# The last down projection with tokens split 282 and 238 instead of 260 and 260

## The chip, the core and the metric

One core of a Trainium2 chip. The metric is the device time of one launch in microseconds (us), as the median of several runs. Engines are named as in the profile: PE is TensorE (PEld its weight loads), DVE is VectorE, ACT is ScalarE, POOL is GpSimd, SP is SyncE, which issues most DMAs.

## The reference

One decoder layer for 512 prompt tokens and 8 single sampled tokens, 520 in all, with 1024 features, in fp32: a feed-forward block (2816 hidden units), a mixer of two parallel head groups, a second feed-forward block, and a final norm. Only the end bears on this change:

```python
def _rms_norm(x, g):
    xf = x.astype(jnp.float32)
    y = xf * lax.rsqrt(jnp.mean(xf * xf, axis=-1, keepdims=True) + EPS)
    return (y * g.astype(jnp.float32)).astype(x.dtype)

def _swiglu(x, wg, wu, wd):
    return (jax.nn.silu(x @ wg) * (x @ wu)) @ wd
...
    h = h + 0.5 * _swiglu(_rms_norm(h, ffn2_norm[l]), ffn2_w_gate[l], ffn2_w_up[l], ffn2_w_down[l])
...
    return _rms_norm(h, final_norm), ...
```

## The kernel before

Features lie on the 128 partitions (1024 features are 8 tiles, `KD`), tokens on the free axis: `h` is 128 x 8 x 520. A product is made of three one-pass matmuls: each operand is split into a rounded high part (type fp32r) and a low part, and `mm3` (L150 to L155) adds high x high, high x low and low x high in PSUM.

The second feed-forward block runs in `stream`: hidden tiles 1 to 21 with gate, up and most of the down projection. What is left at the end is the down projection over the last 6 hidden tiles (16 to 21), done by `down_by_half` (L637): for each of 2 halves of the tokens (`HALVES`, 260 each) and each of 8 output tiles d, a unit of 6 x 3 = 18 matmuls into a PSUM tile `dh_db` (tile d, half b). In the first half the last hidden tile comes late, so units 0 to 5 are begun without it and closed together. PSUM tiles come from two rings of two (tag "BE" for even d, "A" for odd d; tiles 2 and 3 of the first half have banks of their own), so unit (0, 1) needs the bank of `dh_40`, that is DVE must have read it.

Behind each unit `done` (L673) runs: DVE makes `th` = -0.5 x `dh` x r (L677; r is the norm's factor) and adds it to `h` (L679). The `th` tiles take turns in three buffers (tag "ac"). Then `after2` (L837) gathers the final norm: ACT squares the new `h`, DVE adds the square to `acc_last` (`sumsq`, L187 to L194), and ACT scales `h` by the gain into `hg` (L851). The squares (`sq_l`) come from another pool, `tmp`.

`finish(0)` makes the first half's norm, while PE works on the second half: one matmul with ones sums `acc_last` over the partitions on all partitions (`psl`, L873), ACT takes square roots in two pieces (`r_last`, L875, for which ACT loads the table of that function), DVE takes reciprocals (L879), then multiplies `hg` by them in four pieces of two tiles (L883), and SP stores each piece (L885). The second half can't hide its norm, so `finish(1)` puts tokens on partitions: squares as weights against a column of ones give the sums of 65 tokens in each of 4 columns (`psl1`, L864), ACT and DVE make root and reciprocal of 65 x 4 values (`r_tok`, L865, L867), PE transposes them back to all partitions (`factor`, L870), and DVE multiplies and SP stores. The last unit's `th`, `h` and squares are cut in two (`QUARTERS`), and the squares of tiles 6 and 7 (`late`) go to the sums without being added up first.

Each engine runs its own program in order. The order is set at build time by a scheduler that simulates the program; some instructions are pinned to the order of the code (`keep_in_program_order`: the reciprocals, the multiplies of L883, the first matmuls of most units of the second half). While the first units close, DVE and ACT also update the states of the sampled tokens (`hs`, `room`, L1193 and L1195).

Of the kernel before, what the change touches and what calls it, by code (L numbers as in the profile page):

```python
# [10 lines left out]
F32 = mybir.dt.float32  # L11
F32R = mybir.dt.float32r
AF = mybir.ActivationFunctionType
ALU = mybir.AluOpType
# [3 lines left out]
P = 128  # L18
# [3 lines left out]
NT = SEQ + NS  # L22
HB = NT // 2
HALVES = (slice(0, HB), slice(HB, NT))
KD = D // P
FFN = 2816
KF = FFN // P
# [41 lines left out]
def tile_trunk_step(ctx: ExitStack, tc: tile.TileContext, ins: dict, outs: dict):  # L69
    nc = tc.nc  # L70
# [79 lines left out]
    def mm3(ps, whi, wlo, xhi, xlo, start, stop, pin=False, **kw):  # L150
        first = nc.tensor.matmul(ps, whi, xhi, start=start, stop=False, **kw)  # L151
# [3 lines left out]
        nc.tensor.matmul(ps, wlo, xhi, start=False, stop=stop, **kw)  # L155
# [11 lines left out]
    def ws(w, k, m=P):  # L167
        return w[:, k * m : (k + 1) * m]
# [15 lines left out]
                                       op0=ALU.mult, op1=ALU.subtract)  # L184
        sumsq(acc, d, hs, name)

    def sumsq(acc, d, hs, name):  # L187
        n = hs.stop - hs.start
        if d == 0:
            nc.scalar.activation(out=acc[:, hs], in_=h[:, d, hs], func=AF.Square)  # L190
        else:
            sq = tmp.tile([P, HB], F32, tag="ta", name=f"sq_{name}_{d}")
            nc.scalar.activation(out=sq[:, :n], in_=h[:, d, hs], func=AF.Square)
            added[:] = [nc.vector.tensor_tensor(out=acc[:, hs], in0=acc[:, hs], in1=sq[:, :n], op=ALU.add).ins]  # L194

# [75 lines left out]
    class Ffn:  # L271
# [367 lines left out]
        def down_by_half(self, c, lo, after, wd):  # L639
            n = KF - lo  # L640
            banks, units = {}, []
            for d in range(KD):
                if d < STATES[2]:
                    next(self.states)
                src, name = ins[f"w{self.i}d"][d, :, lo * P :], f"{self.i}d{d}_{c}"
                raw = raw_tile(name)[:, : n * P]
                nc.sync.dma_start(out=raw, in_=src)
                if d < 4:
                    home = (wp, 3, ("whi", "wlo")) if d < 2 else (self.wx, 2, ("shi", "slo"))
                    units.append(split(raw, n * P, name, *home))  # L650
                    continue
                hi, lw = (wd.tile([P, n * P], F32R, tag=t, bufs=KD - 4, name=f"{t}_{name}") for t in ("dhi", "dlo"))
                nc.scalar.copy(hi, raw)
                nc.vector.tensor_tensor(out=lw, in0=raw, in1=hi.bitcast(F32), op=ALU.subtract)
                units.append((hi, lw))

            def part(d, b, ks):
                if (d, b) not in banks:
                    if b == 0 and d in (2, 3):
                        banks[d, b] = bank(f"dh{self.i}_{d}{b}")  # L660
                    elif d % 2:
                        banks[d, b] = ps[0].tile([P, 512], F32, tag="A", bufs=2, name=f"dh{self.i}_{d}{b}")
                    else:
                        t = ps[0].tile([P, 2, 512], F32, tag="BE", bufs=2, name=f"dh{self.i}_{d}{b}")
                        banks[d, b] = t[:, 0]
                wh, wl = units[d]
                for k in ks:
                    g = self.g[lo + k]
                    mm3(banks[d, b][:, :HB], ws(wh, k), ws(wl, k), g[:, 0, b], g[:, 1, b], k == 0, k == n - 1,
                        pin=b == 1 and k == 0 and d != 1)  # L670

            def done(d, b):
                hs = HALVES[b]  # L673
                t = self.wx.tile([P, 2, HB], F32, tag="ac", bufs=3, name=f"th{self.i}_{d}{b}")[:, 0]
                for c in QUARTERS if (d, b) == (KD - 1, 1) else (slice(0, HB),):
                    cs = slice(hs.start + c.start, hs.start + c.stop)
                    nc.vector.scalar_tensor_tensor(out=t[:, c], in0=banks[d, b][:, c], scalar=-0.5, in1=self.nx[3][:, cs],  # L677
                                                   op0=ALU.mult, op1=ALU.mult)
                    nc.vector.tensor_tensor(out=h[:, d, cs], in0=t[:, c], in1=h[:, d, cs], op=ALU.add)  # L679
# [90 lines left out]
    f2 = {}  # L770
# [49 lines left out]
    def before2():  # L820
        f2["xt"].release()
        f2["hg"] = pool("hg", "right")
        res.append(f2["hg"].tile([P, KD, NT], F32, tag="hg", name="hg"))
        res.append(f2["hg"].tile([P, HB], F32, tag="rl", name="r_last"))
        res.append(f2["hg"].tile([TQ, 4], F32, tag="rt", name="r_tok"))
# [10 lines left out]
    def after2(d, b, hs):  # L836
        hg = res[0]  # L837
        if (d, b) == (0, 1):
            finish(0)
        elif b and todo:  # L840
            todo.pop(0)()
        if b and d == KD - 2:
            square(d, hs)
        elif b and d == KD - 1:
            for c in QUARTERS:
                square(d, slice(hs.start + c.start, hs.start + c.stop))
        else:
            sumsq(last, d, hs, f"l{d}{b}")
        end = (d, b) == (KD - 1, 1)
        with queued(*((finish(1),) if end else ())):  # L850
            nc.scalar.activation(out=hg[:, d, hs], in_=h[:, d, hs], func=AF.Copy, scale=v("final_norm", d))  # L851
        if end:
            while todo:
                todo.pop(0)()

    def finish(b):
        hs, hg, rl, rt, idt = HALVES[b], *res
        acc = last[:, hs]
        if b:
            sums = bank("psl1")[:TQ, :4]  # L860
            for k, sq in enumerate((acc, late[0], None)):
                for q in range(4):
                    s = late[1 + q // 2][:, q % 2 * TQ :][:, :TQ] if sq is None else sq[:, q * TQ : (q + 1) * TQ]
                    nc.tensor.matmul(sums[:, q : q + 1], s, ones[:, :1], start=(k, q) == (0, 0), stop=(k, q) == (2, 3))  # L864
# [3 lines left out]
            factor = bank("factor")[:, :HB]  # L868
            for q in range(4):
                nc.tensor.transpose(factor[:, q * TQ : (q + 1) * TQ], rt[:, q : q + 1].to_broadcast([TQ, P]), idt)  # L870
        else:
            ps = bank(f"psl{b}")[:, :HB]
            nc.tensor.matmul(ps, ones, acc, start=True, stop=True)  # L873
            for c in QUARTERS:
                nc.scalar.activation(out=rl[:, c], in_=ps[:, c], func=AF.Sqrt, bias=eps, scale=1.0 / D)  # L875
            root, factor = None, rl

        def inverse(q):
            tc.keep_in_program_order(nc.vector.reciprocal(out=rl[:, q], in_=rl[:, q]))  # L879

        def out(d, n):
            tc.keep_in_program_order(
                nc.vector.tensor_tensor(out=hg[:, d : d + n, hs], in0=hg[:, d : d + n, hs],  # L883
                                        in1=factor.unsqueeze(1).to_broadcast([P, n, HB]), op=ALU.mult))
            nc.sync.dma_start(out=outs["y"][:, d : d + n, hs], in_=hg[:, d : d + n, hs])  # L885

        if not b:
            todo.extend([lambda q=q: inverse(q) for q in QUARTERS])
# [597 lines left out]
```

## Time and profile before

| | us |
|---|---|
| median of 3 runs | 954.12 (953.4 to 954.48) |
| span of the profiled execution, first to last instruction | 951.9 |
| what the median has beyond that span | 2.2 |
| PE busy in the span | 942.5 (99%) |
| DVE busy | 852.7 (90%) |
| ACT busy | 635.7 (67%) |

Times in rows are us from the span's start. A row in order of time gives the start, how long it was busy, engine, line, operation, what it writes and reads, the shape, and how many such instructions were put together; in square brackets stands how long the engine was idle before it and who ended that. PE's matmuls overlap in the pipe: each is shown with about 0.28 us, though one starts every 0.12 us.

### The profile page before, as it was taken

The numbers are of one execution on the slowest core, as the hardware profiler recorded it, in microseconds if no ns is written. First come the engines' busy times: TensorE is split into PE (matmuls) and PEld (weight loads), VectorE is DVE, ScalarE is ACT, GpSimd is POOL, SyncE is SP. The second block draws the span as 40 slices with busy tenths as digits, with TensorE's granted clock in tenths as the row PEclk, the third lists the DMA queues.
The fourth block names the chain that finished last, engine by engine and source line by source line (L and its number), as shares of the span: only waits on it lengthen the run. The fifth ranks groups of instructions, "written<-read, shape, count | busy, mean of one in ns | idle before, by whom it ended". The sixth has DMA issues, their size and how long they took to land.

```text
span 951.9 us, 19681 instructions
## 1 busy us (share of the span) xinstructions
PE 942.5 (99%) x7674; PEld 925.9 (97%) x7674; DVE 852.7 (90%) x1462; ACT 635.7 (67%) x1179; POOL 148.3 (16%) x230
## 2 busy tenths in 40 slices
PE   9999999999999999999999999999999999999996
PEld 8999999999999999999999999999999999999996
DVE  6899899998988688789998998999999999999886
ACT  7777756677566455485668735777776676766774
POOL 0011100100100000046251100111112101122120
PEclk9999999999999999999999999999999999999998
DMA  7666554455553343354264453556666655776552
GB/s 205 187 166 150 143 151 135 115 140 156 134 155 95 86 134 122 92 180 138 91 184 133 141 114 115 138 122 160 163 173 176 163 146 144 171 194 185 145 180 91
DMA packets 53995, 138.35 MB, mean 145 GB/s; under 512 B 7750, under 2 KB 15878, under 8 KB 53902
## 3 DMA queue, kind: packets, MB, share of 16 engines
q1 hardware_dynamic: 39918, 104.19, 34.2%
q0 software_dynamic: 13712, 32.78, 18.7%
q8 instruction: 60, 0.98, 0.4%
q14 instruction: 33, 0.27, 0.1%
q10 hardware_dynamic: 272, 0.13, 0.0%
HBM read 129.74 MB, written 7.34 MB: 144 GB/s over the span
## 4 chain that ended last, share of the span: by engine, by line
PE 44%; DVE 2%; issue 1%; POOL 1%; DMA 1%; ACT 1%; DVEq 0%; ACTq 0%; POOLq 0%
PE A L160 8%; PE BE L160 6%; PE wo L160 5%; PE A L165 4%; PE BE L165 3%; PE wo L165 2%; PE P L311 1%; PE dh L155 1%; PE dh L151 1%; PE dh L154 1%; POOL zs L1068 1%; PE inz L151 1%; PE inz L154 1%; PE inz L155 1%; DMA room<-in_state_ssm 1%
## 5 line engine op out<-in xcount | busy, mean ns | idle before, releaser
L504 ACT COPY ac<-A 128x260 f32<-128x260 f32 x85 | 31.6, 372 | 35.4 <-PE A L155 17.3
L433 DVE TENSOR_TENSOR s<-raw 128x1024 f32<-128x1024 f32 x39 | 47.6, 1222 | 4.4 <-DMA raw<-in_w2gu 2.8
L504 ACT COPY ac<-BE 128x260 f32<-128x260 f32 x41 | 15.4, 376 | 33.6 <-PE BE L165 17.7
L151 PE MATMUL inx<-xh_mx,whi_inx 128*128 128x260 f32 x112 | 31.8, 284 | 0.0
L154 PE MATMUL inx<-xl_mx,whi_inx 128*128 128x260 f32 x112 | 31.6, 282 | 0.0
L155 PE MATMUL inx<-xh_mx,wlo_inx 128*128 128x260 f32 x112 | 31.6, 282 | 0.0
L1027 DVE SCALAR_TENSOR_TENSOR A<-U,h,A 128x544 f32<-128x544 f32 x36 | 29.0, 807 | 1.6 <-ACT A L1025 1.2
L311 PE MATMUL P<-x,raw 128*128 128x260 f32 x128 | 28.9, 385 | 0.2 <-DMA raw<-in_w1gu 0.2
L311 PEld LDWEIGHTS P<-x,raw 128*128 128x128 f32 x128 | 24.4, 192 | 4.2 <-DMA raw<-in_w1gu 0.6
L160 PE MATMUL wo<-catg,whi_wo 128*128 128x260 f32 x192 | 27.4, 285 | 0.0
L1193 ACT ACTIVATE so<-br,sxdt 128x128 f32<-128x128 f32 x64 | 22.8, 376 | 5.8 <-DVE room L1195 5.2
L160 PEld LDWEIGHTS wo<-catg,whi_wo 128*128 128x128 f32 x192 | 24.8, 188 | 0.2
L139 ACT CAST thi<-raw 128x1024 fp32r<-128x1024 f32 (+1 forms) x14 | 14.2, 1012 | 15.7 <-PE wo L160 4.8
L1304 DVE TENSOR_TENSOR h<-wo,h 128x260 f32<-128x260 f32 x48 | 19.2, 422 | 5.0 <-PE wo L165 4.7
L252 DVE TENSOR_TENSOR gs<-gq,gs 128x780 fp32r<-128x780 f32 (+1 forms) x28 | 23.3, 831 | 0.0
L151 PE MATMUL inz<-xh_mx,whi_inz 128*128 128x260 f32 x80 | 23.0, 287 | 0.0
L154 PE MATMUL inz<-xl_mx,whi_inz 128*128 128x260 f32 x80 | 22.7, 284 | 0.0
L155 PE MATMUL inz<-xh_mx,wlo_inz 128*128 128x260 f32 x80 | 22.6, 283 | 0.0
L251 ACT CAST gs<-gq 128x780 fp32r<-128x780 f32 (+1 forms) x28 | 20.6, 735 | 1.2 <-DVE gq L555 0.8
L151 PEld LDWEIGHTS inx<-xh_mx,whi_inx 128*128 128x128 f32 x112 | 21.1, 188 | 0.2 <-issue 0.2
L160 PE MATMUL A<-xth_f,qs 128*128 128x260 f32 x84 | 21.2, 283 | 0.0
L160 PE MATMUL A<-xtl_f,qs 128*128 128x260 f32 x84 | 21.2, 284 | 0.0
(3140 smaller groups left out, 4382.9 us busy)
## 6 DMA issues: line engine op xcount, KB each, us to landing
raw<-in_w2gu SPq DMA_DIRECT2D x44, 512.0 KB, 4.4
raw<-in_w1gu SPq DMA_DIRECT2D x41, 512.0 KB, 4.3
raw<-in_w_in SPq DMA_DIRECT2D x24, 512.0 KB, 3.7
raw<-in_w1d SPq DMA_DIRECT2D x16, 512.0 KB, 4.6
raw<-in_w2d SPq DMA_DIRECT2D x16, 512.0 KB, 4.6
raw<-in_w_out SPq DMA_DIRECT2D x12, 512.0 KB, 3.5
ab<-scr_acs SPq DMA_DIRECT2D x8, 512.0 KB, 5.5
h<-in_state_ssm SPq DMA_DIRECT2D x16, 256.0 KB, 3.7
```

Of the source, the lines that this page charges most:

```text
L151: first = nc.tensor.matmul(ps, whi, xhi, start=start, stop=False, **kw)
L154: nc.tensor.matmul(ps, whi, xlo, start=False, stop=False, **kw)
L155: nc.tensor.matmul(ps, wlo, xhi, start=False, stop=stop, **kw)
L160: mm = nc.tensor.matmul(ps, w, x, start=start, stop=False, **kw)
L165: nc.tensor.matmul(ps, w, xhi[k], start=False, stop=k == len(wlo) - 1, **kw)
L251: cast = nc.scalar.copy(hi, s)
L252: low = nc.vector.tensor_tensor(out=lo, in0=s, in1=hi.bitcast(F32), op=ALU.subtract)
L311: mm = nc.tensor.matmul(self.banks[f, u][b][:, :HB], ws(self.raw[f][:, u], j + 4 * q), xg[:, slot[q]], start=j == q == 0, stop=j == 3 and ...
L433: nc.vector.tensor_tensor(out=s1, in0=diag, in1=up0, op=ALU.add)
L504: self.copied = nc.scalar.copy(keep, out[:, :HB]).ins
L1027: nc.vector.scalar_tensor_tensor(out=A[:, :n], in0=U[:, j : j + n], scalar=w(j), in1=A[:, :n], op0=ALU.mult, op1=ALU.add)
L1193: nc.scalar.activation(out=o[:, q], in_=br, func=AF.Copy, scale=sxdt[:, j, b : b + 1]))
```

## The change

The tokens of this last stretch are split into `SPANS`, 282 (`WIDE`) and 238 (`NARROW`), instead of halves of 260; all that runs ahead of it keeps its halves. `TQ` becomes 119, so that the second part fills 2 columns of 119 partitions instead of 4 of 65: the last sums are 6 matmuls instead of 12, the transposes 2 instead of 4. A square of 282 tokens doesn't fit `tmp`'s tiles of 260, so the first part's squares move to the ring of three "ac" buffers that the `th` tiles use.

```diff
+WIDE = 282
+NARROW = NT - WIDE
+SPANS = (slice(0, WIDE), slice(WIDE, NT))
...
-TQ = HB // 4
-QUARTERS = slice(0, HB // 2), slice(HB // 2, HB)
+TQ = NARROW // 2
+QUARTERS = slice(0, TQ), slice(TQ, NARROW)
...
-    def sumsq(acc, d, hs, name):
+    def sumsq(acc, d, hs, name, home=tmp, tag="ta"):
...
-            sq = tmp.tile([P, HB], F32, tag="ta", name=f"sq_{name}_{d}")
+            sq = home.tile([P, HB if home is tmp else NT], F32, tag=tag, name=f"sq_{name}_{d}", **({} if home is tmp else {"bufs": 3}))
...
-                    g = self.g[lo + k]
-                    mm3(banks[d, b][:, :HB], ws(wh, k), ws(wl, k), g[:, 0, b], g[:, 1, b], k == 0, k == n - 1,
-                        pin=b == 1 and k == 0 and d != 1)
+                    g = self.g[lo + k].rearrange("p a b t -> p a (b t)")[:, :, SPANS[b]]
+                    pin = b == 1 and k == 0 and d != 1
+                    mm3(banks[d, b][:, : g.shape[-1]], ws(wh, k), ws(wl, k), g[:, 0], g[:, 1], k == 0, k == n - 1, pin)
...
-                hs = HALVES[b]
-                t = self.wx.tile([P, 2, HB], F32, tag="ac", bufs=3, name=f"th{self.i}_{d}{b}")[:, 0]
-                for c in QUARTERS if (d, b) == (KD - 1, 1) else (slice(0, HB),):
+                hs = SPANS[b]
+                t = self.wx.tile([P, 2, HB], F32, tag="ac", bufs=3, name=f"th{self.i}_{d}{b}").rearrange("p b t -> p (b t)")
+                for c in QUARTERS if (d, b) == (KD - 1, 1) else (slice(0, hs.stop - hs.start),):
...
-            sumsq(last, d, hs, f"l{d}{b}")
+            sumsq(last, d, hs, f"l{d}{b}", *(() if b else (f2["wx"], "ac")))
...
-            sums = bank("psl1")[:TQ, :4]
+            sums = bank("psl1")[:TQ, :2]
             for k, sq in enumerate((acc, late[0], None)):
-                for q in range(4):
-                    s = late[1 + q // 2][:, q % 2 * TQ :][:, :TQ] if sq is None else sq[:, q * TQ : (q + 1) * TQ]
-                    nc.tensor.matmul(sums[:, q : q + 1], s, ones[:, :1], start=(k, q) == (0, 0), stop=(k, q) == (2, 3))
+                for q, c in enumerate(QUARTERS):
+                    s = late[1 + q] if sq is None else sq[:, c]
+                    nc.tensor.matmul(sums[:, q : q + 1], s, ones[:, :1], start=(k, q) == (0, 0), stop=(k, q) == (2, 1))
...
-            for q in range(4):
-                nc.tensor.transpose(factor[:, q * TQ : (q + 1) * TQ], rt[:, q : q + 1].to_broadcast([TQ, P]), idt)
+            for q, c in enumerate(QUARTERS):
+                nc.tensor.transpose(factor[:, c], rt[:, q : q + 1].to_broadcast([TQ, P]), idt)
...
-            for c in QUARTERS:
+            for c in parts:
                 nc.scalar.activation(out=rl[:, c], in_=ps[:, c], func=AF.Sqrt, bias=eps, scale=1.0 / D)
```

`parts` cuts the 282 tokens into two of 141; the sizes of `hg`'s multiplies, of `r_last`, `r_tok` and the identity `idt` follow. The number of matmuls of `down_by_half` stays 2 x 8 x 18, and the scheduler orders the stretch anew.

More of the change, by code (lines that the diff above doesn't have):

```diff
@@ L823, in before2 @@
         res.append(f2["hg"].tile([P, KD, NT], F32, tag="hg", name="hg"))
-        res.append(f2["hg"].tile([P, HB], F32, tag="rl", name="r_last"))
-        res.append(f2["hg"].tile([TQ, 4], F32, tag="rt", name="r_tok"))
+        res.append(f2["hg"].tile([P, WIDE], F32, tag="rl", name="r_last"))
+        res.append(f2["hg"].tile([TQ, 2], F32, tag="rt", name="r_tok"))
         res.append(f2["hg"].tile([TQ, TQ], F32, tag="idt", name="idt"))
@@ L867, in finish @@
             tc.keep_in_program_order(nc.vector.reciprocal(out=rt, in_=rt))
-            factor = bank("factor")[:, :HB]
-            for q in range(4):
-                nc.tensor.transpose(factor[:, q * TQ : (q + 1) * TQ], rt[:, q : q + 1].to_broadcast([TQ, P]), idt)
+            factor = bank("factor")[:, :n0]
+            for q, c in enumerate(QUARTERS):
+                nc.tensor.transpose(factor[:, c], rt[:, q : q + 1].to_broadcast([TQ, P]), idt)
         else:
-            ps = bank(f"psl{b}")[:, :HB]
+            ps = bank(f"psl{b}")[:, :n0]
             nc.tensor.matmul(ps, ones, acc, start=True, stop=True)
-            for c in QUARTERS:
+            for c in parts:
                 nc.scalar.activation(out=rl[:, c], in_=ps[:, c], func=AF.Sqrt, bias=eps, scale=1.0 / D)
@@ L883, in out @@
                 nc.vector.tensor_tensor(out=hg[:, d : d + n, hs], in0=hg[:, d : d + n, hs],
-                                        in1=factor.unsqueeze(1).to_broadcast([P, n, HB]), op=ALU.mult))
+                                        in1=factor.unsqueeze(1).to_broadcast([P, n, n0]), op=ALU.mult))
             nc.sync.dma_start(out=outs["y"][:, d : d + n, hs], in_=hg[:, d : d + n, hs])
         if not b:
-            todo.extend([lambda q=q: inverse(q) for q in QUARTERS])
+            todo.extend([lambda q=q: inverse(q) for q in parts])
         spans = [(1, 2), (3, 2), (5, 2), (7, 1)] if b else [(2, 2), (4, 2), (6, 2)]
```

4 lines of the change are left out of this document (3 added, 1 removed).

## The prediction

> **What bounds the kernel now.** I read the page first, then the busy times by stretch, then the end of the chain that ended last, then the rows of TensorE (PE), VectorE (DVE) and ScalarE (ACT) in order of time, from us 918 to the end.
>
> ```profile
> span 951.9 us, 19681 instructions
> PE 942.5 (99%) x7674; PEld 925.9 (97%) x7674; DVE 852.7 (90%) x1462; ACT 635.7 (67%) x1179; POOL 148.3 (16%) x230
> 904.00:925.00 21.00, 21.00 (x177) 21.00 (x176) 17.55 (x44) 14.58 (x35) 6.42 (x12) 1.00 0.62 203
> 925.00:943.00 18.00, 18.00 (x157) 17.94 (x156) 15.89 (x41) 11.40 (x27) 0.00 (x0) 1.00 0.15 51
> 943.00:946.00 3.00, 1.44 (x19) 1.16 (x18) 1.23 (x6) 1.20 (x4) 0.00 (x0) 1.00 0.26 89
> 942.38 0.13 PE dh L155
> 942.54 0.49 DVE th L677 x2
> 945.38 0.43 DVE hg L883
> 946.41 1.55 DVE hg L883 x3
> ```
>
> After the window come its length and the busy time of PE, weight loads, DVE, ACT and POOL, then the granted clock. PE is busy for all of 904 to 943 at full clock, and the chain lies on its matmuls (`dh`) up to 942.5; behind that it is a relay over DVE, ACT and PE, and the store of the output. So the time is lost or won in two ways: by what moves the start of the last `th` (942.54 now), and by the length of the relay behind it. DVE in 925 to 943 has 15.9 of 18 us, so it is a close second.
>
> **The matmuls.** Their pace, and the nearest other shapes:
>
> ```profile
> 920.33 0.28 PE L151 MATMUL dh<-g,dhi_2d 128*128 128x260 f32 x1
> 924.55 0.28 PE L155 MATMUL dh<-g,dlo_2d 128*128 128x260 f32 x1
> 924.67 0.28 PE L151 MATMUL dh<-g,whi_2d 128*128 128x260 f32 x1
> 940.07 0.28 PE L155 MATMUL dh<-g,dlo_2d 128*128 128x260 f32 x1
> 942.22 0.28 PE L155 MATMUL dh<-g,dlo_2d 128*128 128x260 f32 x1
> 19.76 3.23 PE L311 MATMUL P<-x,raw 128*128 128x260 f32 x14
> 429.46 1.02 PE L1259 MATMUL pst<-xw,bt 128*128 128x512 f32 x2
> L311 PE MATMUL P<-x,raw x128: 382/382/594, 4.6 to 34.0; 128*128 128x260 f32 x128
> L1259 PE MATMUL pst<-xw,bt x16: 590/592/595, 429.5 to 533.6; 128*128 128x512 f32 x16
> L957 PEld LDWEIGHTS dt<-xh_mx,whi_w x16: 120/121/123, 351.8 to 355.9; 128*48 128x48 f32 x16
> L956 PEld LDWEIGHTS dt<-xl_mx,whi_w x14: 94/94/98, 352.1 to 355.7; 128*16 128x16 f32 x14
> L165 PEld LDWEIGHTS A<-xth_f,qs x84: 186/188/193, 625.2 to 911.7; 128*128 128x128 f32 x84
> ```
>
> 18 matmuls of one output tile take 942.22 - 940.07 = 2.15 us, 0.1196 each, and 0.1203 in the first half (920.33 to 924.67 for 36). No row has a one-pass matmul of another width than 260. The unsplit fp32 records go on at (3.23 - 0.382)/13 = 0.219 us for 260 columns and at 1.02 - 0.592 = 0.43 for 512, so 0.84 ns per column; I take half of that for the one-pass form (an estimate): 22 columns are 9.2 ns. So 282 columns cost 0.1295 and 238 cost 0.1104: the wide half takes 144 x 0.0092 = 1.3 us more, the narrow one as much less. Bounds: a pace that doesn't depend on the width (0.12 for both), and, for the narrow form, the fp32 rows, two records of 0.219 per matmul at 260, which is 0.40 at 238.
>
> [...]
>
> **What moves in the order.** VectorE's program in the first half of the tokens, from tile `th_20` on (`th` is the scaled down product, `h` the residual sum, `sq_l` a square that ACT makes of that `h`, `acc_last` its running sum), before:
>
> ```order
> L679 TENSOR_TENSOR h<-th_20_11562,h 128x260
> L677 SCALAR_TENSOR_TENSOR th_30_11588<-dh_30_11569,r_f_7261 128x260
> L677 SCALAR_TENSOR_TENSOR th_40_11614<-dh_40_11595,r_f_7261 128x260
> L194 TENSOR_TENSOR acc_last<-acc_last,sq_l_1_11555 128x260
> L677 SCALAR_TENSOR_TENSOR th_50_11640<-dh_50_11621,r_f_7261 128x260
> L679 TENSOR_TENSOR h<-th_30_11588,h 128x260
> ```
>
> and in the change:
>
> ```order
> L197 TENSOR_TENSOR acc_last<-acc_last,sq_l_1_11555 128x282
> L682 TENSOR_TENSOR h<-th_20_11562,h 128x282
> L680 SCALAR_TENSOR_TENSOR th_30_11588<-dh_30_11569,r_f_7261 128x282
> L197 TENSOR_TENSOR acc_last<-acc_last,sq_l_2_11565 128x282
> L682 TENSOR_TENSOR h<-th_30_11588,h 128x282
> L680 SCALAR_TENSOR_TENSOR th_40_11614<-dh_40_11595,r_f_7261 128x282
> ```
>
> The squares of the first half now share three buffers with the `th` tiles, so each `th` stands behind the sum that frees its buffer: `th_40`, which was taken early to free the PSUM tile of `dh_40`, now has two sums of squares, and so two round trips over ACT, ahead of it.
>
> ScalarE's program in the second half, before (the table of the square root, then the roots `r_last` of the first half, stand ahead of the square of tile 3):
>
> ```order
> L193 ACTIVATE sq_l_2_11777<-h 128x260
> L851 ACTIVATE hg<-h 128x260
> L875 ACT_TABLE_LOAD
> L875 ACTIVATE r_last<-psl_11721,eps 128x130 x2
> L193 ACTIVATE sq_l_3_11805<-h 128x260
> ```
>
> and in the change, where both have moved behind that square, and so behind matmuls of one more output tile:
>
> ```order
> L196 ACTIVATE sq_l_2_11777<-h 128x238
> L854 ACTIVATE hg<-h 128x238
> L196 ACTIVATE sq_l_3_11805<-h 128x238
> L880 ACT_TABLE_LOAD
> L880 ACTIVATE r_last<-psl_11721,eps 128x141 x2
> ```
>
> VectorE waits for those roots with two reciprocals that stand ahead of all its other work of tiles 4 to 7, in both programs.
>
> **The first half, by rows.**
>
> ```profile
> 919.01 0.28 PE L155 MATMUL dh<-g,wlo_2d 128*128 128x260 f32 x1
> 919.59 0.76 DVE L677 SCALAR_TENSOR_TENSOR th<-dh,r_f 128x260 f32<-128x260 f32 x2
> 920.86 0.87 DVE L1195 SCALAR_TENSOR_TENSOR hs<-hs,sdec,so 128x128 f32<-128x128 f32 x3
> 923.45 0.76 DVE L677 SCALAR_TENSOR_TENSOR th<-dh,r_f 128x260 f32<-128x260 f32 x2
> 932.04 0.43 DVE L679 TENSOR_TENSOR h<-th,h 128x260 f32<-128x260 f32 x1
> 932.56 0.42 ACT L193 ACTIVATE sq_l<-h 128x260 f32<-128x260 f32 x1 [1.40 <-DVE h L679]
> 933.02 0.43 DVE L194 TENSOR_TENSOR acc_last<-acc_last,sq_l 128x260 f32<-128x260 f32 x1 [0.55 <-ACT sq_l L193]
> ```
>
> A VectorE instruction on 260 columns holds the engine 0.34 us (0.76 - 0.42), its result is there after 0.43; 22 columns are 0.023, so 0.36 for 282 and 0.315 for 238; a state update (`hs`) holds it (0.87 - 0.347)/2 = 0.26. From the end of an `h` to ACT's start go 0.09, the square takes 0.42, and 0.04 later DVE can add it. Now `dh_40` is freed at 924.2 (the second of the two `th` at 923.45), and PE needs that tile at 924.67: 0.45 to spare, no wait. With the change, `dh_00` is complete after some 98 wider matmuls, at 919.29 + 0.9, and `th_00` starts at 920.3. Ahead of `th_20` stand 4 instructions of 0.36 and 6 of 0.26: 923.3. From there a tile takes 1.36 (0.45 for `h`, 0.09, 0.43 and 0.03 over ACT, 0.36 for the sum): `th_40` starts at 926.05 and is done at 926.5. PE, 1.3 us later by its wider matmuls, gets there at 926.0: it waits about 0.55 us and begins the narrow half at 926.55 instead of 924.67.
>
> **The second half.**
>
> ```profile
> 932.89 0.50 ACT L851 ACTIVATE hg<-h 128x260 f32<-128x260 f32 x1
> 933.40 1.28 ACT L875 ACT_TABLE_LOAD   x1
> 934.70 0.63 ACT L875 ACTIVATE r_last<-psl,eps 128x130 f32<-128x130 f32 x2
> 935.10 1.79 DVE L879 RECIPROCAL r_last<-r_last 128x130 f32<-128x130 f32 x2 [0.71 <-ACT r_last L875]
> 936.81 0.37 DVE L194 TENSOR_TENSOR acc_last<-acc_last,sq_l 128x260 f32<-128x260 f32 x1
> 937.42 0.69 DVE L883 TENSOR_TENSOR hg<-hg,r_last 128x520 f32<-128x520 f32 x1
> 938.03 0.42 DVE L679 TENSOR_TENSOR h<-th,h 128x260 f32<-128x260 f32 x1
> 942.54 0.49 DVE L677 SCALAR_TENSOR_TENSOR th<-dh,r_f 128x130 f32<-128x130 f32 x2 [0.22 <-PE dh L155]
> ```
>
> From 936.81 DVE has no gap until it waits 0.22 us for PE ahead of the last `th`: that 0.22 is all the slack there is behind the reciprocals. With the change: tile 3 is complete on PE at 926.55 + 72 x 0.1106 (0.1104 and what the records add) + 0.17 = 934.7. DVE does `th`, a sum and `h` (0.315 + 0.315 + 0.40): 935.75. ACT squares 0.09 later, 0.40: 936.25; the table 1.28: 937.55; first root 0.38: 937.95. The reciprocals start at 938.0 instead of 935.1 and take 1.71 x 141/130 = 1.85: 939.85. The load was hidden behind PE's work for tile 3 and loses that cover. Then DVE has 8 instructions of 0.315 and 4 of 0.655 (564 columns; 520 took 0.61), 5.14 us, to the last `th`: **945.0**. PE has its last matmul done at 943.15, so DVE decides, 2.45 us later than now.
>
> **The relay behind it.**
>
> ```profile
> 943.33 0.54 ACT L834 ACTIVATE sq_last<-h 128x130 f32<-128x130 f32 x2 [0.70 <-DVE h L679]
> 943.69 0.63 PE L864 MATMUL psl<-ones,sq_last 128*65 128x1 f32 x8 [0.30 <-ACT sq_last L834]
> 944.93 0.42 PE L870 MATMUL factor<-idt,r_tok 65*128 65x65 f32 x4 [0.60 <-PE psl L864]
> 945.38 2.58 DVE L883 TENSOR_TENSOR hg<-hg,factor 128x260 f32<-128x260 f32 x5 [0.56 <-PE factor L870]
> out_y<-hg SPq DMA_DIRECT2D x7, 260.0 KB, 2.3
> ```
>
> Four shorter `th`/`h` and the square save 0.05. Sums of 119-column weights: half as many records, each nearly twice as long (0.63 for 8 of 65 now); I take 0.03 saved, between a gain of 0.3 if a record costs the same and a loss of 0.1. Two transposes of 119 for four of 65: 0.05 saved. The last multiplies lose 8 x 22 columns at 1.04 ns, 0.18, and the stores 8% of their bytes, 0.05. Together 0.35 (0.1 to 0.7). The first half's stores grow to 282 KB and start 2.5 us later, but four of them and the last five stay in SP's order; I cost that at nothing, up to 0.3 if the DMAs back up at the end. The bigger identity (119 x 119) is loaded early, at nothing.
>
> **Sum.** +2.45 - 0.35 = +2.1 us: span 954.0. The median of the runs, 954.12, is 2.2 above the profiled span; with the same 2.2 the time is **956.2 us**, +0.22%. About 0.2%, 1.9 us, is what a measurement of this kernel can tell from no change, so the forecast stands just beyond it.
>
> **Rivals.**
> - *The roots come in time* (not slower). Place: ACT between `hg` of tile 2 and the table load. If the load could run while ACT is idle, from about 934.8, the roots would come at 936.1, the reciprocals end at 938.35 and the last `th` start at 943.5: 954.7 us. It decides at 938.0: if the reciprocals end before that, PE ends last (943.15) and the relay's gain gives 954.4. Against it: the load stands behind the square in ACT's program, and before it began 0.01 us after the instruction ahead of it. 12%.
> - *Narrow matmuls lose the one-pass pace* (much slower). If 238 columns cost 0.40, PE runs 72 matmuls to tile 3 and 72 behind it: the last `th` at 984.5, the time 995.8 us. No row speaks for it except that every one-pass matmul of this kernel has 260 columns. 11%.
> - *Flat or cheap pace*, inside my case: narrow at 0.12 gives 945.65 and 956.9; wide at 0.12 and narrow at 0.1095 (in proportion) 944.5 and 955.7.
>
> **How the numbers follow.** My case has 77%: from 955.2 to 957.2, its middle at 956.2, with three fifths of it above 956.03 (954.12 + 0.2%). So slower has 0.46 + 0.11, rounded to 0.56; same 0.31 + 0.12, less 0.03 for faster by a gain I don't see: 0.41. The range 954.6 to 957.3 takes in my case with its bounds and the first rival, and leaves out the slow pace.
>
> **What would show it.** Right: PE idle about 0.5 us ahead of its first 238-column matmul; table load near 936.3, reciprocals from 938.0; DVE without a gap from there to 945; PE idle some 2 us ahead of the last sums; the store's relay 0.35 shorter. Wrong: matmuls of 238 columns at another pace than 0.11; a table load that starts ahead of the square's end; PE still waited for by the last `th`.

## The result, and the profile after

The changed kernel takes 955.88 us (median of 18 runs, 955.03 to 958.82); the kernel before, on the same chip, 954.10 (18 runs, 953.40 to 956.97). The ratio is 1.0020 with a 95% interval of 1.0013 to 1.0026: slower by 1.9 us (1.2 to 2.5) by that ratio, while the two medians differ by 1.78. The forecast was 956.2 us, slower by 2.1. The profiled execution took 957.18 us, 1.3 above the median, with a span of 955.4.

The page of the changed kernel, and its busy time by stretch (columns as before: PE, weight loads, DVE, ACT, POOL, then the granted clock):

```profile
span 955.4 us, 19652 instructions
PE 944.2 (99%) x7660; PEld 926.4 (97%) x7660; DVE 852.4 (89%) x1462; ACT 636.2 (67%) x1179; POOL 148.6 (16%) x230
```

```profile
904.00:925.00 21.00, 21.00 (x165) 21.00 (x165) 15.52 (x36) 13.69 (x32) 6.43 (x12) 1.00 0.60 197
925.00:943.00 18.00, 17.82 (x154) 17.50 (x153) 14.61 (x37) 11.03 (x26) 0.00 (x0) 1.00 0.05 20
943.00:946.00 3.00, 1.91 (x17) 1.63 (x15) 3.00 (x9) 1.40 (x4) 0.00 (x0) 1.00 0.76 252
946.00:949.20 3.20, 2.00 (x10) 1.48 (x10) 0.89 (x6) 1.33 (x5) 0.00 (x0) 0.66 0.30 106
```

PE loses a little of 925 to 943 (17.82 of 18.00; 18.00 before), DVE fills all of 943 to 946 (3.00; 1.23 before), and the last row has a granted clock of 0.66. The chain that ended last no longer runs over the matmuls up to their end. It goes over the `th` that PE waits for at the start of the narrow part, the first narrow matmuls, up to tile 3 at 935.5, then the square of that tile, the table load and the reciprocals:

```profile
926.79 0.45 DVE th L680
927.28 0.38 PE dh L154
...
936.80 0.40 ACT sq_l L196
937.22 1.28 ACT L880
938.93 1.94 DVE r_last L884 x2
946.97 0.96 PE psl L869 x4
950.15 1.43 DVE hg L888 x3
```

Its rows on PE, from the last wide tile to the end:

```profile
924.07 0.29 PE L158 MATMUL dh<-g,dlo_2d 128*128 128x282 f32 x1
...
926.82 0.29 PE L158 MATMUL dh<-g,dlo_2d 128*128 128x282 f32 x1
927.28 0.38 PE L154 MATMUL dh<-g,whi_2d 128*128 128x238 f32 x1 [0.18 <-DVE th L680]
...
941.88 0.27 PE L158 MATMUL dh<-g,dlo_2d 128*128 128x238 f32 x1
...
943.89 0.28 PE L158 MATMUL dh<-g,dlo_2d 128*128 128x238 f32 x1
945.03 0.58 PE L869 MATMUL psl<-ones,acc_last 128*119 128x1 f32 x4 [0.86 <-DVE acc_last L197]
945.84 0.58 PE L869 MATMUL psl<-ones,sq_last 128*119 128x1 f32 x4 [0.23 <-ACT sq_last L837]
946.97 0.95 PE L869 MATMUL psl<-ones,sq_last 128*119 128x1 f32 x4 [0.55 <-ACT sq_last L837]
948.52 0.63 PE L875 MATMUL factor<-idt,r_tok 119*128 119x119 f32 x2 [0.60 <-PE psl L869]
```

21 matmuls of 282 columns lie between the first two rows, (926.82 - 924.07)/21 = 0.131 us each; 18 of 238 columns between 941.88 and 943.89, 0.112 each. The first narrow matmul starts 0.46 behind the one ahead of it and waits for a `th`. The last one starts at 943.89, and PE then idles until 945.03.

On ACT and on DVE:

```profile
936.80 0.40 ACT L196 ACTIVATE sq_l<-h 128x238 f32<-128x238 f32 x1 [1.27 <-DVE h L682]
937.22 1.28 ACT L880 ACT_TABLE_LOAD   x1
938.52 0.65 ACT L880 ACTIVATE r_last<-psl,eps 128x141 f32<-128x141 f32 x2
```

```profile
938.93 1.94 DVE L884 RECIPROCAL r_last<-r_last 128x141 f32<-128x141 f32 x2 [1.29 <-ACT r_last L880]
940.78 0.34 DVE L680 SCALAR_TENSOR_TENSOR th<-dh,r_f 128x238 f32<-128x238 f32 x1
...
945.21 0.74 DVE L888 TENSOR_TENSOR hg<-hg,r_last 128x564 f32<-128x564 f32 x1
945.87 0.46 DVE L680 SCALAR_TENSOR_TENSOR th<-dh,r_f 128x119 f32<-128x119 f32 x2
...
949.19 2.39 DVE L888 TENSOR_TENSOR hg<-hg,factor 128x238 f32<-128x238 f32 x5 [0.77 <-PE factor L875]
```

The table load follows the square of tile 3 within 0.02 us of its end, the reciprocals wait 1.29 us for the roots behind it, and from there the rows of DVE carry no idle time up to the last `th`, which starts 1.98 us after PE's last matmul (0.32 before: 942.54 against 942.22).

**One ruler for all profiles.** Whole times scatter by some us between executions, and most of that lies ahead of the down stretch: its first `dh` matmul starts anywhere between 904.28 and 908.55 us in the fourteen profiles. So everything below is counted from the start of the stretch's first `dh` matmul (904.46 in the profile before, 905.15 here; both rows begin so):

| profile | first dh | last dh | last th | first last multiply | end | end, against before |
|---|---|---|---|---|---|---|
| before | 904.46 | 37.76 | 38.08 | 40.92 | 47.45 | |
| before, second profile | 904.75 | 37.76 | 38.08 | 40.92 | 47.39 | -0.06 |
| changed | 905.15 | 38.74 | 40.71 | 44.03 | 50.25 | +2.80 |
| changed, second profile | 905.00 | 38.75 | 40.73 | 43.44 | 49.60 | +2.15 |

Starts are given behind the first `dh` in us; the end is that of the span (951.91 and 955.40 in the first and third row). "Relay" below is the time from the last `th` to the first of the last multiplies, "tail" from there to the end.

### The profile page after: what moved, and what is told of

Its sections match the earlier page's. It is cut to its first block, busy times and chain, and to the rows that moved or that the text cites. A ratio compares the mean times of both kernels' runs of the same rounds, so it can differ in the third digit from the quotient of the medians.

```text
span 955.4 us, 19652 instructions
## 1 busy us (share of the span) xinstructions
PE 944.2 (99%) x7660; PEld 926.4 (97%) x7660; DVE 852.4 (89%) x1462; ACT 636.2 (67%) x1179; POOL 148.6 (16%) x230
## 4 chain that ended last, share of the span: by engine, by line
PE 89%; DVE 4%; issue 3%; ACT 2%; DMA 1%; POOL 1%; DVEq 0%; SPq 0%; POOLq 0%; ACTq 0%
PE A L163 8%; PE BE L163 6%; PE wo L163 5%; PE P L314 4%; PE A L168 4%; PE A L154 4%; PE A L158 4%; PE A L157 4%; PE BE L168 3%; PE BE L154 3%; PE BE L157 3%; PE BE L158 3%; PE wo L168 2%; PE inx L154 1%; PE inz L154 1%
## 5 line engine op out<-in xcount | busy, mean ns | idle before, releaser
L507 ACT COPY ac<-BE 128x260 f32<-128x260 f32 x41 | 15.4, 377 | 33.5 <-PE BE L168 16.6
L154 PE MATMUL inx<-xh_mx,whi_inx 128*128 128x260 f32 x112 | 31.8, 284 | 0.0
L158 PEld LDWEIGHTS inx<-xh_mx,wlo_inx 128*128 128x128 f32 x112 | 21.1, 188 | 0.0
```

What stands on the lines that cost most here:

```text
L507: self.copied = nc.scalar.copy(keep, out[:, :HB]).ins
```

## The experiments

The table's second and fourth row are two of them, and set the scale. First the kernel before, profiled again:

> The kernel before a second time, for a second profile. Theory: the stretch from the first matmul of the down stretch to the end takes 47.4 to 47.5 us again, whatever the whole execution takes, since nothing in it waits for a transfer; rival: it scatters as the whole time does, by 1 us or more, and then single profiles can't carry differences of a few tenths.

Measured: 47.39 against 47.45, with each of the three marks ahead of the end equal to 0.01 us. These two executions hardly differ as a whole (spans of 952.1 and 951.9 us), so this pair alone doesn't rule out that the stretch scatters with the whole. The run `warm6` below speaks against that: its stretch begins 3.55 us later than that of the changed kernel's second profile (908.55 against 905.00) and takes 49.60 like that one. A tenth of a us in the stretch can be read.

The changed kernel again:

> The changed kernel itself a second time, beside the other runs of this group. Theory (TensorE's clock falls at a time that is set by when it rose at the start of the program, 942.08 us earlier in the first profile, and not by the work at the end): the stretch from the first matmul of the down stretch to the end takes 50.25 us if the fall lies ahead of the last sums again, and 49.85 us if it lies behind them; nothing else in the stretch moves by more than 0.1 us. Rival (the half clock belongs to the kernel): last th to first last multiply is 3.32 us again, wherever the fall lies. Time about 956.0.

Measured: ratio 1.0025 (1.0016 to 1.0035), PE and the last `th` as in the first profile, but a relay of 2.71 instead of 3.32 us. Its PE rows and its clock by stretch, and the clock of the first profile:

```profile
946.84 0.58 PE L869 MATMUL psl<-ones,sq_last 128*119 128x1 f32 x4 [0.55 <-ACT sq_last L837]
948.02 0.39 PE L875 MATMUL factor<-idt,r_tok 119*128 119x119 f32 x2 [0.60 <-PE psl L869]
```

```profile
946.00:948.00 2.00, 0.87 (x7) 0.71 (x7) 0.75 (x5) 1.10 (x5) 0.00 (x0) 1.00 0.42 147
948.00:950.00 2.00, 0.39 (x2) 0.18 (x2) 1.56 (x4) 0.10 (x1) 0.00 (x0) 0.58 0.10 34
```

```profile
946.00:948.00 2.00, 1.37 (x8) 1.20 (x8) 0.71 (x4) 0.73 (x4) 0.00 (x0) 0.75 0.48 170
948.00:950.00 2.00, 0.63 (x2) 0.29 (x2) 0.98 (x3) 0.60 (x2) 0.00 (x0) 0.50 0.00 0
```

With the clock at 1.00, the last four records of the sums take 0.58 and the transposes 0.39; in the first profile the clock fell to 0.50 in the middle of the stretch 946 to 948 (mean 0.75), and they took 0.95 and 0.63. The theory's 49.85 was for the transposes slow and the sums not; here both were spared, so the stretch came out at 49.60. The rival, that the half clock belongs to the kernel, is out.

### The table load alone

A root of one column, whose result nobody reads, takes the load ahead of the first part's last square:

```diff
         else:
+            if (d, b) == (KD - 1, 0):
+                spare = f2["hg"].tile([P, 1], F32, tag="sp", name="spare")
+                nc.scalar.activation(out=spare, in_=last[:, :1], func=AF.Sqrt, bias=eps, scale=1.0 / D)
             sumsq(last, d, hs, f"l{d}{b}", *(() if b else (f2["wx"], "ac")))
```

> Theory (order on the activation engine, with a gapless vector engine behind it): the changed kernel loads the square-root table behind the square of the first part's tile 3, so its two roots end 1.3 us later than they could, and the vector engine runs from them without a gap to the last th. Here a root of one column, whose result nobody reads, is issued ahead of the square of the first part's last tile and takes the table load with it. Expected: no table load behind the last roots' tile any more, the reciprocals about 1.3 us earlier, the last th and the end about 1.0 to 1.3 us earlier, near 954.7 us. Rival (the ring of three buffers, or the matmul widths, set the end): the last th stays where it is and the time stays at 955.9 us. Second rival: TensorE's last matmul, 1.98 us ahead of the last th in the profile, becomes the bound only if more than that is won, so it can't hide the gain.

Measured: ratio 1.0011 (1.0003 to 1.0020). Marks 38.74, 39.33, 42.28, end 48.51. ACT and DVE:

```profile
932.74 1.28 ACT L853 ACT_TABLE_LOAD   x1
...
937.62 0.41 ACT L196 ACTIVATE sq_l<-h 128x238 f32<-128x238 f32 x1 [0.51 <-DVE h L682]
937.93 0.63 ACT L883 ACTIVATE r_last<-psl,eps 128x141 f32<-128x141 f32 x2
```

```profile
938.39 1.93 DVE L887 RECIPROCAL r_last<-r_last 128x141 f32<-128x141 f32 x2
...
945.32 0.46 DVE L680 SCALAR_TENSOR_TENSOR th<-dh,r_f 128x119 f32<-128x119 f32 x2
```

The roots stand right behind the square of tile 3, the reciprocals no longer wait, and the last `th` is 1.38 us earlier (39.33 against 40.71) while PE is where it was (38.74). That is a little more than half of what the change cost at that mark (1.38 of 2.63), from one instruction's place. The rival (ring or widths set the end) predicted no move. The stretch is still 1.06 us longer than before, and so is the time: 955.43, where theory had 954.7, beside 954.70 for the kernel before in these runs.

### The ring alone, and its removal

In the kernel before, only the squares of the first half are put into the ring of three `ac` buffers:

```diff
-            sumsq(last, d, hs, f"l{d}{b}")
+            sumsq(last, d, hs, f"l{d}{b}", *(() if b else (f2["wx"], "ac")))
```

> The kernel before with one part of the change alone: the first half's squares come from the ring of three that th uses; halves of 260, the sums on four columns of 65 partitions and the table load are left as they were. Theory: the ring puts the second half's first th behind two sums and their squares, TensorE waits some 0.6 to 1.4 us ahead of the second half's first units, and because the vector engine has only 0.2 us of slack behind the reciprocals the end moves by 0.5 to 1.4 us: 954.6 to 955.5. Rival (the ring is harmless, the loss comes from widths and the order of the table load): 954.1, within 0.2.

Measured: ratio 1.0012 (1.0004 to 1.0021). Marks 38.75, 39.07, 41.91, end 48.39. The rows of PE where the second half begins:

```profile
926.60 0.28 PE L155 MATMUL dh<-g,dlo_2d 128*128 128x260 f32 x1
927.59 0.39 PE L151 MATMUL dh<-g,whi_2d 128*128 128x260 f32 x1 [0.71 <-DVE th L677]
```

From start to start 0.99 us, where the kernel before has 0.12 (924.55 to 924.67), and the last `dh` and `th` are both 0.99 later. So the ring costs by itself, the more as PE is not slowed by wide matmuls on the way there.

Now the changed kernel, with two buffers for those squares instead of the ring:

```diff
-            sq = home.tile([P, HB if home is tmp else NT], F32, tag=tag, name=f"sq_{name}_{d}", **({} if home is tmp else {"bufs": 3}))
+            sq = home.tile([P, HB if home is tmp else WIDE], F32, tag=tag, name=f"sq_{name}_{d}", **({} if home is tmp else {"bufs": 2}))
...
-            sumsq(last, d, hs, f"l{d}{b}", *(() if b else (f2["wx"], "ac")))
+            sumsq(last, d, hs, f"l{d}{b}", *(() if b else (f2["hg"], "sx")))
```

> The first part's squares get two buffers of their own; the ring of three is left to the th tiles as in the kernel before. Theory (ring and order both, the order of the table load with the gapless vector engine decides): TensorE's wait of about 0.6 us ahead of the first narrow unit goes, but the table load still stands behind the square of tile 3 and the roots move by no more than about 0.5 us, so the time falls by 0.3 to 0.6 us, to about 955.4. Rival (the ring is the whole loss): all of it goes, 953.8 to 954.2 us. Second rival (the wait is covered and free): 955.9, no change.

Measured: ratio 1.0028 (1.0015 to 1.0041), no gain. Marks 38.32, 40.66, 43.61, end 49.85. PE's wait is gone and its last matmul is 0.42 earlier, but the last `th` moves by 0.05 only. ACT shows why:

```profile
935.61 0.40 ACT L196 ACTIVATE sq_l<-h 128x238 f32<-128x238 f32 x1 [0.92 <-DVE h L682]
935.91 0.48 ACT L854 ACTIVATE hg<-h 128x238 f32<-128x238 f32 x1
936.41 1.28 ACT L880 ACT_TABLE_LOAD   x1
```

The square of tile 3 comes 0.42 earlier too (31.23 us behind the first `dh`, 31.65 in the changed kernel), so what PE gains does reach ACT. But the new order puts the `hg` of that tile ahead of the load, which costs 0.40, and the load starts where it did (32.03 against 32.07). The theory's half us did not come out. Its second rival, that the wait is covered and free, has the number right, but the run doesn't show it: two things changed, and they cancel. With ACT's order kept, the gain might have come through; that was not run. (The end is 0.40 earlier than in the first profile of the changed kernel mostly because the sums ran at full clock, the last four records in 0.58 instead of 0.95: the relay is 2.95 instead of 3.32.)

### Both at once

Own buffers and the early load together, in short:

```diff
+                nc.scalar.activation(out=spare, in_=last[:, :1], func=AF.Sqrt, bias=eps, scale=1.0 / D)
-            sumsq(last, d, hs, f"l{d}{b}", *(() if b else (f2["wx"], "ac")))
+            sumsq(last, d, hs, f"l{d}{b}", *(() if b else (f2["hg"], "sx")))
```

> The changed kernel with two buffers for the first part's squares alone, and with the one-column root that takes the table load ahead. In the profiles, own buffers alone took 0.42 us from TensorE's part of the stretch and left the last th where it was; the early load alone took 1.38 us from the last th and left TensorE as it was. Theory (each hides the other, and what then is left is the matmul widths, 0.56 us): TensorE's last matmul starts 38.3 us behind the first of the stretch, the last th some 0.4 us later, and the stretch takes 47.8 to 48.2 us, 0.3 to 0.8 more than in the kernel before (47.45); time 0.4 to 0.8 us above the kernel before. Rival (the two don't add, the vector engine has too much to do in any order): last th not below 39.2, stretch 48.4 or more.

Measured: ratio 1.0009 (1.0000 to 1.0018). Marks 38.27, 38.58, 42.33, end 48.51. Theory right for PE and the last `th`, rival right for the end, though not by its mark: the last `th` is only 0.50 later than before, but the relay takes 3.74 us. DVE at the end:

```profile
943.15 0.47 DVE L680 SCALAR_TENSOR_TENSOR th<-dh,r_f 128x119 f32<-128x119 f32 x2
943.53 0.40 DVE L682 TENSOR_TENSOR h<-th,h 128x238 f32<-128x238 f32 x1
943.85 0.74 DVE L891 TENSOR_TENSOR hg<-hg,r_last 128x564 f32<-128x564 f32 x1
944.50 0.47 DVE L682 TENSOR_TENSOR h<-th,h 128x119 f32<-128x119 f32 x2
```

Between the last `th` and its own `h` stand an `h` and a multiply, 0.97 us, that DVE has not got done before. The reciprocals begin at 937.43, 32.86 us behind the first `dh`, where the kernel before has 30.64, and the four multiplies that DVE has to fit in ahead of the end come behind them. Of these 2.22 us the wider matmuls give some 144 x (0.131 - 0.120) = 1.6 (an estimate). Another part is the experiment's own: the added root reads `acc_last`, and the last two sums of the wide part, which write it, now wait for that root:

```profile
934.12 0.77 DVE L197 TENSOR_TENSOR acc_last<-acc_last,sq_l 128x282 f32<-128x282 f32 x2 [0.49 <-ACT spare L853]
...
937.11 0.41 DVE L680 SCALAR_TENSOR_TENSOR th<-dh,r_f 128x238 f32<-128x238 f32 x1 [0.52 <-PE dh L158]
```

The two sums stand 29.55 us behind the first `dh`; with own buffers alone they stand at 28.40. And in DVE's order the reciprocals now follow the `th` of the second row, which waits 0.52 us for PE. So the run shows that this order leaves too much for DVE behind the roots, but not that parts of 282 and 238 do so in any order: a root that reads another tile was not tried.

### The order alone, in the kernel before

The first try issued the first half's roots, reciprocals and first multiply later in the program, and left ACT's order as it was:

```diff
-        elif b and todo:
+        elif b and todo and d > 3:
             todo.pop(0)()
...
+            if (d, b) == (3, 1):
+                roots.pop()()
+                for _ in range(3):
+                    todo.pop(0)()
...
-            for c in QUARTERS:
-                nc.scalar.activation(out=rl[:, c], in_=ps[:, c], func=AF.Sqrt, bias=eps, scale=1.0 / D)
+            def take():
+                for c in QUARTERS:
+                    nc.scalar.activation(out=rl[:, c], in_=ps[:, c], func=AF.Sqrt, bias=eps, scale=1.0 / D)
+
+            roots.append(take)
```

> The kernel before (halves of 260, squares in their own tiles, four columns), with one thing changed: the first half's two roots, and with them the table load, are issued behind the square of tile 3 of the second half, and their reciprocals and multiplies follow them. Theory (the order alone costs): TensorE keeps its time (last matmul 37.8 us behind the stretch's first), the reciprocals start 2 to 3.5 us later than in the kernel before, the vector engine then runs to the last th without a gap, the last th falls 1.5 to 3 us later and the stretch takes 49.0 to 50.5 us instead of 47.45. Rival (without the ring and the narrow part the vector engine has room, and the order is hidden): 47.4 to 47.8 us, no difference in the time.

Measured: ratio 1.0000 (0.9991 to 1.0009). Marks 37.76, 38.35, 41.18, end 47.67. The table load starts 28.95 us behind the first `dh`, to 0.01 us where it did: the roots kept their place ahead of the square of tile 3, so this run does not test the order on ACT. Only the reciprocals moved, behind one more sum, from 30.64 to 31.56; of these 0.92 us DVE's slack took up all but 0.27 at the last `th`. In the second try the roots are held behind the square:

```diff
+                with queued(root_behind[0]):
                     roots.pop()()
```

> The kernel before with one exchange on the activation engine, the one that the change makes there too: the square of the second half's tile 3 stands ahead of the table load and the two roots instead of behind them (and its sum ahead of the reciprocals instead of behind them). Ring, widths and columns are those of the kernel before. Theory (the order alone costs, less the slack that this kernel has): tile 3's h ends near 934.4 in the clock of the first profile, so square, load and roots follow from there and the reciprocals start at 936.5 instead of 935.10, 1.4 us later; one sum of 0.34 us is already done by then and 0.3 us of waiting for TensorE goes, so the last th is 0.75 us later; TensorE is as before (37.76). The stretch takes 48.0 to 48.4 us instead of 47.45. Rival (the order is free as long as neither ring nor widths delay anything): 47.4 to 47.6.

Measured: ratio 1.0009 (0.9998 to 1.0019). Marks 37.76, 38.96, 42.05, end 48.50.

```profile
935.96 0.42 ACT L193 ACTIVATE sq_l<-h 128x260 f32<-128x260 f32 x1 [1.10 <-DVE h L679]
936.40 1.28 ACT L881 ACT_TABLE_LOAD   x1
937.69 0.63 ACT L881 ACTIVATE r_last<-psl,eps 128x130 f32<-128x130 f32 x2
```

```profile
938.10 1.79 DVE L887 RECIPROCAL r_last<-r_last 128x130 f32<-128x130 f32 x2 [1.25 <-ACT r_last L881]
...
944.89 0.48 DVE L677 SCALAR_TENSOR_TENSOR th<-dh,r_f 128x130 f32<-128x130 f32 x2
```

Reciprocals 1.53 us later (32.17 against 30.64), DVE without a gap, the last `th` 0.88 later, PE untouched. The order costs by itself, in a kernel with neither ring nor wide part; the rival is out. The time of the whole doesn't resolve it (the interval takes in 1). The end is 0.1 above the range, by a relay of 3.09 whose transposes fell into the half clock (0.62 in 947 to 948).

### Other widths

```diff
-WIDE = 282
+WIDE = 264
```

> The changed kernel with parts of 264 and 256 tokens in place of 282 and 238 (two columns of 128 partitions); the ring stays, and the table load stands ahead of the square of the first part's tile 3 again. Theory (ring and order): the ring's wait stays, TensorE's last matmul near 38.8 us behind the stretch's first, the last th 0.3 to 0.6 us behind it, and the stretch takes 48.2 to 48.7 us, about 1 us more than before and 1.5 to 2 less than the changed kernel. Rival (the narrow part and its columns set the loss, not the order): between both in proportion to the widths, 4 of 22 columns: 47.9 us; and if the division has nothing to do with it, 50.2 us as in the changed kernel.

Measured: ratio 1.0005 (0.9994 to 1.0015). Marks 38.40, 38.72, 41.51, end 47.86, lower than the theory said. The ring's wait is there, but it moves PE by 0.64 us and not by 0.99, and the load stands ahead of the square of tile 3 again, so DVE keeps up (last `th` 0.32 behind PE, as before). The number fits the rival better (47.9 by the widths' proportion), the marks the theory: what is left against the kernel before lies at PE, ahead of the last `th`.

With the squares' own buffers and the early load on top of that:

```diff
-WIDE = 282
+WIDE = 264
...
+                nc.scalar.activation(out=spare, in_=last[:, :1], func=AF.Sqrt, bias=eps, scale=1.0 / D)
-            sumsq(last, d, hs, f"l{d}{b}", *(() if b else (f2["wx"], "ac")))
+            sumsq(last, d, hs, f"l{d}{b}", *(() if b else (f2["hg"], "sx")))
```

> All that the runs so far point to in one kernel: parts of 264 and 256 (two columns of 128 partitions), two buffers of their own for the first part's squares, and the one-column root that takes the table load ahead. Theory: no wait of TensorE at the start of the second part, last matmul 37.8 to 38.0 us behind the stretch's first, last th 0.3 us behind it, relay 2.7 to 2.85 and tail 6.35 us: the stretch takes 47.2 to 47.5 us, that is at best 0.2 us under the kernel before, and the times of the two can't be told apart. Rival (as with parts of 282 and 238, the vector engine ends up with too much behind the roots): relay 3.2 or more, stretch 48 us or more.

Measured: ratio 1.0005 (0.9996 to 1.0013). Marks 37.68, 38.47, 41.25, end 47.59, just above the theory's range: PE 0.08 earlier than before, but DVE 0.78 behind it, relay 2.78, tail 6.34. The added root holds up sums here too (DVE waits 0.38 us for it ahead of the last two wide ones), and the reciprocals begin at 31.99 instead of 31.16. In parts of 264 and 256 the load already stood in a good place, so the root may have cost more than it gave; own buffers without it were not run. No version of the split that was run beats the kernel before.

### The clock

12 fp32 matmuls of ones, whose result nobody reads, are pinned between the last `dh` and the sums; then 6 of them:

```diff
             sums = bank("psl1")[:TQ, :2]
+            idle = idle_bank()
+            for _ in range(12):
+                tc.keep_in_program_order(nc.tensor.matmul(idle[:, :P], ones, ones, start=True, stop=True))
```

> Adds 12 fp32 matmuls of ones by ones, 128 columns, whose result nobody reads, on TensorE between the last matmul of the down stretch and the sums with tokens on partitions. Theory (the relay behind the last th was 0.6 us longer than forecast because TensorE, idle since 944.2, fell to half its clock at 946.97): with the clock held, the last matmuls of the sums again stand 0.104 us apart instead of 0.200, the two transposes some 0.10 instead of 0.22, and last th to first last multiply goes from 3.32 to 2.7 to 2.9 us; the end comes 0.4 to 0.6 us earlier, near 955.4 us. Rival (the clock is only a bystander, the relay waits for its inputs): the stretch stays within 0.1 us of 3.32 and the time at 955.9. Third: the added matmuls themselves get in the way of the first sums, which shows as a wait of the sums behind them and a time above 955.9.

Measured: ratio 1.0029 (1.0017 to 1.0040). Marks 38.76, 40.74, 44.37, end 50.58.

```profile
944.12 2.84 PE L871 MATMUL idle<-ones 128*128 128x128 f32 x24
946.80 0.48 PE L875 MATMUL psl<-ones,acc_last 128*119 128x1 f32 x4
947.14 0.76 PE L875 MATMUL psl<-ones,sq_last 128*119 128x1 f32 x6
```

The third case: 24 records of 0.11 us hold PE until 946.8 and push all sums behind them; the relay is 3.64 us, with the clock at 1.00 for the sums (946 to 948). With 6:

```diff
-            for _ in range(12):
+            for _ in range(6):
```

> The changed kernel with 6 in place of 12 fp32 matmuls of ones behind the down stretch's last matmul: they end near 945.5, before the last squares are there. [...]

Measured: relay 2.71, end 49.60, the same as the second profile of the changed kernel, which has no added matmul; ratio 1.0032 (1.0021 to 1.0042) beside 1.0025 (1.0016 to 1.0035) for the changed kernel in the same group, so no gain in the time. In that profile the clock stayed up to 948.31 with nothing added, so this run does not show that the added matmuls held it.

## Why the prediction was right

- **Matmul pace.** Forecast 0.1295 and 0.1104 us for 282 and 238 columns, measured 0.131 and 0.112. The wide part costs 144 x (0.1310 - 0.1203) = 1.54 us, the narrow one gives back 144 x (0.1196 - 0.1117) = 1.14, where I had 1.3 both ways. So PE ends later than I had it (last `dh` +0.98 us, forecast +0.64). That end is not what the last `th` waits for, so this error hardly reached the sum. The slow narrow pace is out. No run shows matmuls fast enough for the lower end of my case, 955.2 us; what they have is 0.131 and 0.112.
- **The ring.** Forecast: PE waits 0.55 us at its first narrow matmuls. Measured: the first starts 0.46 and the second 0.22 us behind the one ahead, 0.44 more than two matmuls at pace; without the ring PE's last matmul is 0.42 earlier. Right in mechanism, a little less in size. The start of the narrow part, which this `th` sets, came as forecast: 22.13 us behind the first `dh`, forecast 22.09 (926.55 - 904.46). The wait lies on the chain that ended last, and where it was taken away, the order on ACT moved with it and took the gain back.
- **The order on ACT and DVE.** Forecast: table load behind the square of tile 3, DVE without a gap to the last `th`, +2.45 us. Measured +2.63 and +2.65 in the two profiles. The steps came as forecast, each 0.2 to 0.3 late: counted from the first `dh`, table load 32.07 (forecast 31.8), reciprocals 33.78 (33.5), last `th` 40.71 (40.5). The early load gave 1.38 of the 2.63 back; the exchange in the kernel before cost 0.88. Most of the rest goes with PE's later marks, which the sum had as the later start of the narrow half. Own buffers and early load together leave 0.50 at the last `th`, but pay 0.90 in the relay.
- **The relay, the term that was mis-sized.** Forecast -0.35 for relay and tail together. First profile: relay 3.32 against 2.84, tail 6.22 against 6.53, so +0.17. Second: 2.71 and 6.16, so -0.50 (-0.13 and -0.37). The tail gained 0.31 and 0.37, forecast 0.23, so the stores, costed at nothing, cost nothing that shows; the relay of the second profile, -0.13, is what the terms for it add up to. The term that was mis-sized in the first profile is the relay, +0.48 instead of -0.13. It priced every record of the sums and transposes at full clock: "the granted clock" of PE stands in the rows of the profile before, 1.00 up to 946, and I did not ask where it would fall once the relay came 2 us later.
- **Sum.** Forecast +2.1, measured +2.15 in the profile with the clock up and +2.80 in the other; the runs say 1.9 (1.2 to 2.5). That 2.15 comes so close to 2.1 is in part luck: the last `th` came 0.20 later than forecast and relay and tail gained 0.15 more. The stretch of the second profile, 2.15 of 954.1 or 0.23%, lies inside both intervals measured, that of the first, 0.29%, inside only the one of the second group. How many executions have the clock fall within the relay is not known.

The rival that the roots come in time is out by the rows of ACT (load 0.02 us behind the square).

Taken apart at the last `th`, +2.63: PE +0.98, of it 0.42 the ring and 0.56 the widths (own buffers against before); DVE behind PE +1.66, of it 1.38 the table load's place. This is an account by marks: the ring's 0.42 also delays the square that the load follows, so the parts can't be taken away one by one.

## What to carry to other kernels

A change of tile widths moves more than its matmuls: look up where each engine's order puts the one instruction that others wait for, here a table load of 1.28 us that had stood in the shadow of the next tile's matmuls and was moved behind its square. A change that takes a wait away can also move an instruction: own buffers gave PE 0.42 us, and an `hg` that the new order put ahead of the load took 0.40 back, so look at the order again behind each change. One column of the right function, issued early, gave 1.38 of 2.63 us back at the last `th`; but what an added instruction reads can hold up others, as this one's input did with the sums. And compare stretches from a common first instruction: whole times scattered by 3 to 5 us, the stretch of the kernel before repeated to 0.06 us.

## What the runs showed of the hardware

The moment at which PE's clock falls at the end, from 1.00 to 0.50, did not follow the last matmuls. The trace's record has full clock from 4.93 to 947.01 us in the first profile of the changed kernel, from 6.23 to 948.31 in the second, and from 4.98 to 947.06 in the first of the kernel before, whose last `dh` starts 1.67 us earlier than that of the changed kernel (942.22 against 943.89): 942.08 us in all three, and in all but two of the fourteen profiles. The ring's and that of 6 added matmuls have 945.49; what made it longer there was not shown. A fall also came behind dense work: in the run with the early load PE was busy for 1.87 of the 2.00 us from 944 to 946 and for 0.58 of the next 1.00, and the clock fell at 947.49. What sets the moment, these runs don't show.

One-pass matmuls of other widths than 260 keep close to a line: 0.112, 0.120 and 0.131 us at 238, 260 and 282 columns, 0.44 ns per column from end to end ((130.9 - 111.7)/44). Before, no row of this kernel had shown one.
